# One layer of a hybrid attention and recurrence block on one core: the whole program issued from one list schedule, with twelve more pairs of weight blocks in the seven-product form

## The chip, the cores and the metric

The kernel runs on one core of one Trainium2 chip. The time is device microseconds (us) of one launch, and the figure that counts is the median over the runs. The engines are named as the profile names them: PE (TensorE, matrix products; PEld are its weight loads, which overlap), DVE (VectorE), ACT (ScalarE), POOL (GpSimd) and SP (SyncE, which issues transfers). All arithmetic is float32 or a split form of it, and a matrix product is seen in the profile as many MATMUL instructions of 128 rows by 512 columns.

## The reference

For 256 tokens of width 2048 and one layer:

```python
h = rmsnorm(x, norm1_gain[l])
proj = h @ w_in[l]                          # 2048 x 7168: q k v | q f i g
attn = chunk_band_attention(q_a, k_a, v_a, rel_bias[l])   # 8 heads, chunks of 64
attn = rmsnorm(attn, attn_out_gain[l])
rec = hgrn2_mixer(q_r, f_r, i_r, g_r, lb_all[l], grn_norm_gain[l])
x = x + concatenate([attn, rec]) @ w_out[l]               # 2048 x 2048
h2 = rmsnorm(x, norm2_gain[l])
ff = silu(h2 @ w_gate[l]) * (h2 @ w_up[l])                # two of 2048 x 5632
x = x + ff @ w_down[l]                                    # 5632 x 2048
return rmsnorm(x, final_gain)
```

Only the five large products matter for the change; the mixers between them are small.

## The kernel before

**Three products for one.** Every large product is made at float32 precision from float32r operands. A weight tile `raw` is split into `wh` (ACT, a copy into float32r, L89) and `wl` (DVE, `raw - wh`, L90); the activations are held split in the same way (`hx`, `h`, `fh`/`fl`). A product is then three MATMULs into the same PSUM bank: high by high, high by low, low by high (`Group.mul`, L337).

**Groups, pairs and kinds.** The weights come from HBM in chunks of 1 MB (128 x 2048 float32, `raw`, three buffers): one chunk is a *pair*, 2 x 2 blocks of 128 rows by 512 columns. A group computes a 256 x 1024 piece of the output and runs over pairs: 8 pairs for the input projections in natural layout, for the output projection and for each of the eleven gate and up groups (`Gated`), 22 pairs for each of the two groups of the down projection (`Down`). A pair has one of three kinds:

- `d`: eight block products, 24 MATMULs. Four blocks are split, which is two `wh` and two `wl` of 1024 columns.
- `s`: seven block products in Winograd's form, 21 MATMULs. DVE first makes four sums of weight blocks in `ta` (1024 columns, L386) and `tb` (two of 512, L387 and L388), then splits the three plain blocks and the four sums: `wl` once at 512 columns and three times at 1024. The activations need four sums of their own (`row_sums`, L291: tiles `wsa`, `wsb`, `hs`, `sf`, `sx`), made once for each pair that some group runs in this form.
- `a`: eight products, without DVE. ACT writes `low = -wh` (L356), then a transfer on the queue of POOL adds the same weights from HBM to it (L357), so that `low` becomes the low part. Such a pair has two adding transfers of 512 KB and a raw buffer of its own (`rawa`).

The four tiles `wh` and four `wl` of 1024 columns are shared by all pairs, so the split of one pair runs about one pair ahead of PE.

**Gate and up.** The first group is eight `d`; the other ten run `a4 s0 d5 s1 a6 s2 s3 d7` (L1032). After its last pair a group's eight PSUM banks are combined by DVE (`spread`, `block`), and the product of gate and up is transposed on PE and split into `fh` and `fl` (`ff_split`).

**Down.** The first group has 7 `s` pairs of 22, the second 9 (`FAST`, L1145). The sums of the activations are made two pairs at a time (`sum_pairs`) in the first three gaps between pairs, and the last three alone.

**What sets the order.** The code is written group by group: while PE runs a pair, the next one is prepared (`run_groups`). The tile framework's scheduler then moves instructions on each engine as their operands allow; a few are pinned to the program's order with `keep_in_program_order` (L219, L298, L348, L356). Buffers come from pools (`wraw`, `wsp`, `dn`, `pacc`, `paux` and others) that rotate them. All plain loads stand in one queue on SP, in the order written.

```python
    full = [("a", 4), ("s", 0), ("d", 5), ("s", 1), ("a", 6), ("s", 2), ("s", 3), ("d", 7)]
    down = [Down(g, order_of(KP, list(range(FAST if g else FAST - 2)), 1 if g else 6, 2), w_down, ...)
```

Of the kernel before, what the change touches and what calls it, by code (L numbers as in the profile page):

```python
# [7 lines left out]

F32 = mybir.dt.float32
F32R = mybir.dt.float32r  # L10
# [6 lines left out]
P = 128  # L17
S = 256
# [11 lines left out]
FAST = 9  # L30
FASTU = 4
BANKS = ("c00", "c01", "c10", "c11", "m1", "m5", "m6", "m7")
# [10 lines left out]


@with_exitstack
def hybrid_block(ctx: ExitStack, tc: tile.TileContext, x, xT, w_in, w_out, w_gu, w_down,
                 bias, gains, lbnd, fgain, out):
    nc = tc.nc

    const = ctx.enter_context(tc.tile_pool(name="const", bufs=1))  # L50
    wraw = ctx.enter_context(tc.tile_pool(name="wraw", bufs=3))
    wsp = ctx.enter_context(tc.tile_pool(name="wsp", bufs=4))
    ev = ctx.enter_context(tc.tile_pool(name="ev", bufs=2))
    act_t = ctx.enter_context(tc.tile_pool(name="act_t", bufs=1))
    res = ctx.enter_context(tc.tile_pool(name="res", bufs=1))
    small = ctx.enter_context(tc.tile_pool(name="small", bufs=2))
    pacc = ctx.enter_context(tc.tile_pool(name="pacc", bufs=4, space=PSUM))
    paux = ctx.enter_context(tc.tile_pool(name="paux", bufs=4, space=PSUM))
# [22 lines left out]

    def dma(o, i):
        with ExitStack() as st:
            if prev:
                st.enter_context(tc.issue_after(prev[-1]))
            prev.append(nc.sync.dma_start(o, i).ins)

# [8 lines left out]
    def rstd_of(sums, n, cnt, tag, space=None):  # L96
        if space is None:
            space = small.tile([P, 3, n], F32, tag=tag, name=tag)
# [23 lines left out]
    def split_chunk(raw, kn, wn, pieces=1):  # L122
        parts = []
        for hf in range(2):
            wh = wsp.tile([P, 2 * W], F32R, tag="wh", name="wh")
            wl = wsp.tile([P, 2 * W], F32R, tag="wl", name="wl")
# [8 lines left out]
    def load_chunk(src, idx, pieces=1):  # L135
        raw = wraw.tile([P, KC * W], F32, tag="raw", name="raw")
# [5 lines left out]
    def tr_product(src, chunk, rhs):  # L142
        ps = [pacc.tile([P, 2, S], F32, tag="acc", name="acc") for _ in range(2)]
# [15 lines left out]
    def tr_evac(dst, ps, rows, pool, bufs=2):  # L159
        for m in range(2):  # L160
            tb = pool.tile([P, S], F32, tag="tb", name="tb", bufs=bufs)
# [4 lines left out]
    dn = ctx.enter_context(tc.tile_pool(name="dn", bufs=1))  # L166
    wsa = tc.tile_pool(name="wsa", bufs=1)
    own = {"wsa": wsa.__enter__().tile([P, 2, 4, 2, P], F32R, name="wsa")}
    mix = tc.tile_pool(name="mix", bufs=1)
    mixp = mix.__enter__()  # L170
    ab = tc.tile_pool(name="ab", bufs=1)
    abp = ab.__enter__()

    def t4(shape, name):
        return abp.tile(shape, F32, tag="t4", name=name, bufs=NT4)

    hx = act_t.tile([P, KD, 2, S], F32R, tag="hx", name="hx")
    xr = [t4([P, 4, S], "xr") for _ in range(4)]
    nc.gpsimd.memset(ones, 1.0 / 1024.0)
    wm = paux.tile([P, P], F32, tag="aux", name="wm")  # L180
# [4 lines left out]
    make_identity(nc, ident)  # L185
# [6 lines left out]
    aT = []  # L192
    for t in range(NT):
        a = abp.tile([P, 4, P], F32, name=f"aT{t}")
        nc.gpsimd.memset(a, 0.0)
        aT.append(a)
# [12 lines left out]
    ma = mixp.tile([P, 2, 8, S], F32R, name="ma")  # L209
    kx = mixp.tile([P, 2, 2, 4, S], F32R, tag="mr", name="kx")  # L210
    rst1 = const.tile([P, NT], F32, name="rst1")
    G = res.tile([P, H, 384], F32, tag="res", name="G")
# [3 lines left out]
    def x_squares(c):  # L216
        sq = t4([P, 4, S], "sq")
        k = 0 if c else 1
        tc.keep_in_program_order(nc.scalar.activation(sq[:, k:4, :], xr[c][:, k:4, :], AF.Square))  # L219
# [9 lines left out]
    def row_rstd(dst, cols):  # L229
        pr = paux.tile([P, S], F32, tag="aux", name="prow")  # L230
        for t in range(NT):
            dg = ev.tile([P, P], F32, tag="junk", name="dg")
# [4 lines left out]
    def first_rstd():  # L237
        pr = paux.tile([P, NT], F32, tag="aux", name="pr1")
# [5 lines left out]
    def lower_bound():  # L244
        mx = small.tile([P, H], F32, tag="lbm", name="lbm", bufs=1)
        e = small.tile([P, 2, H], F32, tag="lbe", name="lbe")
# [22 lines left out]
    def transposed(nm, dst):  # L269
        tr_evac(dst, tr_product(w_in, chunk_of(nm), hx), R1, abp)  # L270
# [20 lines left out]
    def row_sums(dst, hi, lo, in_order=False):  # L291
# [5 lines left out]
        if in_order:  # L297
            tc.keep_in_program_order(first)  # L298
# [930 lines left out]
```

## Time and profile before

| | |
|---|---|
| three runs, us | 1131.49, 1131.65, 1132.62; median 1131.65 |
| span of the profiled execution | 1129.3 us, 14420 instructions |
| PE busy | 1119.4 us (99%) |
| PE weight loads busy | 936.2 us (83%) |
| DVE busy | 986.8 us (87%) |
| ACT busy | 724.1 us (64%) |
| POOL busy | 45.9 us (4%) |
| read from HBM | 245.92 MB |

The span runs from the first to the last instruction of the one execution that was profiled; the runs are timed from outside, and their median is 2.35 us above that span. No time of the profiled execution other than its span is given. By the first products that read their operands, the output projection begins at about 335 us, gate and up at about 426 us and the down projection at 891 us; the last product ends at 1121 us. Before them lie the input projections with the two mixers. A busy time is the union of an engine's instructions with their latencies, so an instruction that starts before the one ahead of it has ended is not counted twice, and the distance between two starts is less than one duration.

### The profile page before, as it was taken

How to read it: one execution, taken by the hardware profiler on the slowest of the kernel's cores; microseconds unless marked ns; L12 is line 12 of the kernel's file. 1: busy time of each engine (PE TensorE's matmuls, PEld its weight loads, DVE VectorE, ACT ScalarE, POOL GpSimd, SP SyncE). 2: the span in 40 equal slices, each digit the busy share in tenths (PEclk: the TensorE clock that was granted, in tenths of full speed). 3: DMA queues.
4: the chain of work that ended last, by engine and by line, in shares of the span. 5: the costliest groups of instructions: out<-in, count | busy, mean ns of one | idle time of the engine just before them, and what ended most of it. 6: DMA issues, size and time to landing. Idle time of an engine off the chain costs nothing.

```text
span 1129.3 us, 14420 instructions
## 1 busy us (share of the span) xinstructions
PE 1119.4 (99%) x5344; PEld 936.2 (83%) x5344; DVE 986.8 (87%) x1294; ACT 724.1 (64%) x930; POOL 45.9 (4%) x73
## 2 busy tenths in 40 slices
PE   9999999999999999999999999999999999999997
PEld 7888888888888888888888888888888888888885
DVE  7867778996999998789989989989989999898986
ACT  8555566575866666676676676676766565555563
POOL 0000000000000000000000010010010000000000
PEclk9999999999999999999999999999999999999999
DMA  8665544656455668778778878788788755655652
GB/s 337 217 214 186 185 149 150 223 191 257 149 187 187 223 203 319 223 223 229 268 251 240 266 244 251 263 238 258 250 244 252 289 192 216 223 187 190 220 189 109
DMA packets 40246, 251.05 MB, mean 222 GB/s; under 512 B 4592, under 2 KB 5104, under 8 KB 13424
## 3 DMA queue, kind: packets, MB, share of 16 engines
q1 hardware_dynamic: 32832, 220.51, 53.3%
q0 software_dynamic: 7200, 29.36, 13.4%
q8 instruction: 42, 0.69, 0.2%
q10 hardware_dynamic: 144, 0.26, 0.1%
q14 instruction: 28, 0.23, 0.1%
HBM read 245.92 MB, written 4.19 MB: 221 GB/s over the span
## 4 chain that ended last, share of the span: by engine, by line
PE 96%; DVE 2%; ACT 1%; DMA 0%; issue 0%; SPq 0%; ACTq 0%
PE c L337 62%; PE m L337 16%; PE acc L151 11%; PE acc L154 5%; PE ptr L282 1%; DVE wl L90 1%; PE po L793 0%; PE pa L766 0%; DMA GX<-in_gains_dram 0%; ACT wh L89 0%; PE pp L518 0%; DVE oo L807 0%; PE po L795 0%; PE pc L773 0%; PE sc L498 0%
## 5 line engine op out<-in xcount | busy, mean ns | idle before, releaser
L89 ACT ACTIVATE wh<-raw 128x1024 fp32r<-128x1024 f32 (+1 forms) x368 | 351.7, 971 | 182.1 <-PE c L337 84.1
L90 DVE TENSOR_TENSOR wl<-raw,wh 128x1024 fp32r<-128x1024 f32 (+1 forms) x368 | 403.4, 1113 | 72.6 <-ACT wh L89 71.6
L337 PE MATMUL c<-wh,h 128*128 128x512 f32 x928 | 274.2, 390 | 0.0
L337 PEld LDWEIGHTS c<-wh,h 128*128 128x128 f32 x928 | 174.2, 188 | 36.6 <-DVE ff L1011 0.3
L151 PE MATMUL acc<-hx,wh 128*128 128x512 f32 x512 | 162.2, 397 | 0.0
L89 ACT ACTIVATE wh<-ta 128x1024 fp32r<-128x1024 f32 x66 | 70.1, 1061 | 88.0 <-PE c L337 46.3
L337 PE MATMUL c<-wl,h 128*128 128x512 f32 x304 | 119.4, 393 | 0.0
L89 ACT ACTIVATE wh<-tb 128x1024 fp32r<-128x1024 f32 x66 | 70.0, 1061 | 71.0 <-PE c L337 38.8
L154 PEld LDWEIGHTS acc<-hx,wl 128*128 128x128 f32 x512 | 96.2, 188 | 22.5
L337 PE MATMUL c<-wh,hx 128*128 128x512 f32 x336 | 105.5, 392 | 0.2 <-DVE hx L628 0.2
L154 PE MATMUL acc<-hx,wl 128*128 128x256 f32 x512 | 100.7, 278 | 0.0
L90 DVE TENSOR_TENSOR wl<-ta,wh 128x1024 fp32r<-128x1024 f32 x66 | 80.7, 1223 | 18.8 <-ACT wh L89 18.8
L90 DVE TENSOR_TENSOR wl<-tb,wh 128x1024 fp32r<-128x1024 f32 x66 | 80.6, 1222 | 11.8 <-ACT wh L89 9.2
L337 PE MATMUL c<-wh,fh 128*128 128x512 f32 x224 | 87.3, 390 | 0.2 <-DVE ff L1003 0.2
L337 PE MATMUL c<-wh,fl 128*128 128x512 f32 x224 | 87.2, 389 | 0.0
L337 PE MATMUL c<-wl,fh 128*128 128x512 f32 x224 | 87.1, 389 | 0.0
L386 DVE TENSOR_TENSOR ta<-raw 128x1024 f32<-128x1024 f32 x66 | 80.7, 1222 | 1.7 <-DMA raw<-in_w_down_dram 0.9
L337 PE MATMUL m<-wh,hs 128*128 128x512 f32 x240 | 81.8, 389 | 0.0
L151 PEld LDWEIGHTS acc<-hx,wh 128*128 128x128 f32 x512 | 78.4, 189 | 0.1
L337 PEld LDWEIGHTS c<-wh,hx 128*128 128x128 f32 x336 | 63.2, 188 | 13.6 <-ACT wh L89 0.5
L337 PEld LDWEIGHTS c<-wl,h 128*128 128x128 f32 x304 | 57.1, 188 | 14.0 <-DVE wl L90 2.5
L337 PE MATMUL c<-wl,hx 128*128 128x512 f32 x168 | 64.8, 391 | 0.0
(353 smaller groups left out, 1730.9 us busy)
## 6 DMA issues: line engine op xcount, KB each, us to landing
raw<-in_w_gu_dram SPq DMA_DIRECT2D x68, 1024.0 KB, 6.8
raw<-in_w_in_dram SPq DMA_DIRECT2D x54, 1024.0 KB, 4.8
raw<-in_w_down_dram SPq DMA_DIRECT2D x44, 1024.0 KB, 4.8
rawa<-in_w_gu_dram SPq DMA_DIRECT2D x20, 1024.0 KB, 6.1
low<-in_w_gu_dram POOLq DMA_DIRECT2D x40, 512.0 KB, 6.9
raw<-in_w_out_dram SPq DMA_DIRECT2D x14, 1024.0 KB, 4.8
x<-in_x_dram SPq DMA_DIRECT2D x2, 1024.0 KB, 7.9
rawa<-in_w_out_dram POOLq DMA_DIRECT2D x2, 1024.0 KB, 7.1
```

The lines of the kernel that those rows point to most:

```text
L89: nc.scalar.activation(hi, src, AF.Copy)
L90: nc.vector.tensor_tensor(lo, src, hi.bitcast(F32), ALU.subtract)
L151: nc.tensor.matmul(ps[m].rearrange("p j t -> p (j t)"), lhsT=wh[:, cols[m]], rhs=both, start=kt == 0, stop=False)
L154: nc.tensor.matmul(ps[m][:, 0, :], lhsT=wl[:, cols[m]], rhs=rhs[:, kt, 0, :], start=False, stop=kt == KD - 1)
L282: nc.tensor.transpose(pt[:, j, t, :], nat(t)[:, n0 + j * P:n0 + (j + 1) * P], ident)
L337: nc.tensor.matmul(self.bank[n], lhsT=a, rhs=b, start=self.left[n] == self.total[n], stop=self.left[n] == 1)
L386: nc.vector.tensor_tensor(ta, raw[:, 1:3], raw[:, 0:2], ALU.subtract)
```

## The change

**One list schedule.** All operations from the first memset of `aT` on are no longer issued as the code runs. Stand-ins for the engines (`Taken`) record each in a list (`Plan.add`) with an estimated duration and with the places that it reads and writes. When the list is complete, `Plan.order` plays it through at build time: PE takes the first ready one of the next 48 in its list, DVE and ACT the ready one that is due first (counted back from the end), SP and POOL keep the order written. The program is then issued in the order of these starts with the framework's own scheduler off (`manual_schedule`). Buffers are no longer drawn from pools but from fixed places (`Places`, `fixed`, `turn`).

**Five raw buffers.** From the output projection to the end of gate and up, `raw0` to `raw2` are joined by two more of 1 MB, `more`; `rawa` is gone. The down projection has three again.

**More seven-product pairs.** A new kind `b` is the seven-product form in which the low part of the two plain blocks `b22` and `b21` is made by one adding transfer as in `a`, instead of by DVE. Gate and up groups 1 to 8 run `a5 s0 b1 s2 a6 s3 b4 d7`: five seven-product pairs and six adding transfers instead of four and four. Group 9 has five seven-product pairs and four transfers, group 10 four and none. A fifth pair's activation sums are kept in the still empty end of `fh` (`hs5`), and the added low parts go to `low`, of which there is one buffer, and to the still empty ends of `fh` and `fl`. That is 9 more pairs. In the down projection 9 and 10 pairs instead of 7 and 9 are of the form, 3 more. There the activation sums are made one pair at a time (`sum_pair`), the fourth sum in the place of a block that the pair no longer needs.

```diff
+    def add(self, engine, what, emit, out, ins, kind="w", own=(), func=None):
+        busy, done = self.cost(engine, what, out, ins, func)
...
+        self.ops.append((engine, busy, done, size, emit, set(), func if func in self.OWN else None, touched))
...
+        with self.tc.manual_schedule(engines={E.PE, E.DVE, E.Activation, E.Pool}):
+            for i in self.order():
+                self.ops[i][4]()
...
+            b22, b21 = self.added_half(raw, low, 1) if kind == "b" else halves_of(raw[:, 2:4])
...
         def prepare(i):
             gr, n = todo[i]
-            nxt, m = todo[i + 1] if i + 1 < len(todo) else (None, 0)
-            begins = nxt is not None and nxt.items[m][0] == "a"
-            if begins:
-                nxt.begin(nxt.items[m][1])
-                nxt.lower(0)
...
+            kind, j = gr.items[n]
+            if kind in "ab":
+                gr.begin_ahead(j)
+            for k in {"a": (0, 1), "b": (1,)}.get(kind, ()):
+                gr.lower(j, k)
+            return gr.prepare(kind, j)
...
+                fixed["raw"] += [new(f"more{i}", [P, KC * W], F32, "more") for i in range(2)]
...
-    full = [("a", 4), ("s", 0), ("d", 5), ("s", 1), ("a", 6), ("s", 2), ("s", 3), ("d", 7)]
+    orders = ["d0 d1 d2 d3 d4 d5 d6 d7"] + 8 * ["a5 s0 b1 s2 a6 s3 b4 d7"] + ["a5 s0 b1 s2 b3 s4 d6 d7", "d4 s0 d5 s1 d6 s2 s3 d7"]
...
-        def sum_pairs(self, j, n):
-            ks, js = slice(2 * j, 2 * j + 2 * n), slice(j % 2, j % 2 + n)
-            row_sums((sf[:, j // 2] if j < FAST - 1 else own["sx"])[:, :, :, js, :], fh[:, ks, :], fl[:, ks, :])
+        def sum_pair(self, j):
+            ks = slice(2 * j, 2 * j + 2)
+            s, k = (sf, j) if j < FAST - 1 else (own["sx"], 0)
+            ff = turn("ff")
+            sm = form_sums(fh[:, ks, :], fl[:, ks, :], ff[:, 0].rearrange("p (a b c) -> p a b c", a=1, b=2),
+                           ff[:, 1].rearrange("p (a b c) -> p a b c", a=4, b=1))
+            split(s[:, 0, :, k, :], s[:, 1, :, k, :], sm[:, 0:3, 0])
+            split(fh[:, 2 * j, P:S], fl[:, 2 * j, P:S], sm[:, 3, 0])
...
-    down = [Down(g, order_of(KP, list(range(FAST if g else FAST - 2)), 1 if g else 6, 2), w_down, g * KP, f_of, s_of)
-            for g in range(2)]
+    kinds = "ddd" + 9 * "sd" + "d", "d" + 8 * "sd" + "ssddd"
+    down = [Down(g, fast_first(kinds[g]), w_down, g * KP, f_of, s_of) for g in range(2)]
```

Over the whole program the built instructions change as follows: PE has 4394 MATMULs of 512 columns instead of 4430, the shorter ones are the same; DVE has 1380 instructions instead of 1292, among them 42 more of 512 columns, 6 more of 1024, 42 more of 128, 10 more of 384 and 12 fewer of 256; ACT has 21 more of 1024 columns, 30 more that are shorter and 22 loads of a function table instead of 17; POOL issues 56 adding transfers instead of 44. In the changed program nearly all rows carry line 336, that of the stand-in, so the tiles tell them apart; `bank` is a PSUM bank.

**How it moves on ACT in a gate and up group.** Before, both `low` of an `a` pair (tile `low`, from `rawa`) are written shortly before the pair's own high parts (`wh<-rawa`):

```order
L992 COPY ff<-m_6544 128x512
L356 ACTIVATE low<-rawa 128x1024
L89 ACTIVATE wh<-raw 128x1024 x2
L356 ACTIVATE low<-rawa 128x1024
L366 ACTIVATE wh<-rawa 128x1024 x2
L1009 ACTIVATE ff<-ff,rst_2804 128x512
```

Now the low parts (tiles `fl`, `low` and `fh` by where they are kept, from `raw` or `more`) stand singly among the splits of pairs that come earlier:

```order
L336 ACTIVATE wh_80<-more 128x1024
L336 ACTIVATE fl<-raw_76 128x1024
L336 ACTIVATE wh_82<-tb 128x1024
L336 ACTIVATE fl<-raw_76 128x1024
L336 ACTIVATE wh_79<-more 128x512
L336 ACTIVATE wh_80<-more 128x1024
L336 ACTIVATE wh_81<-ta 128x1024
L336 ACTIVATE wh_82<-tb 128x1024
L336 ACTIVATE wh_79<-raw_78 128x1024
L336 ACTIVATE wh_80<-raw_78 128x1024
L336 COPY ff<-bank_95 128x512
L336 ACTIVATE wh_81<-raw_76 128x1024
```

The two `fl` are one `a` pair's; ten other ACT instructions and more now stand between them and the pair's high parts, so an adding transfer is issued two to three pairs before it is used.

**How it moves on DVE at the start of the down projection.** Before, the activation sums (`a`, `sm`, then the low part `sf`) of two pairs at a time stand among the splits of `d` pairs, whose only DVE work is `wl<-raw,wh`:

```order
L295 TENSOR_TENSOR a<-fh,fl 128x1024
L90 TENSOR_TENSOR wl<-raw,wh 128x1024
L300 TENSOR_TENSOR sm<-a 128x256
L302 TENSOR_TENSOR sm<-a 128x256
L301 TENSOR_TENSOR sm<-sm,a 128x256
L303 TENSOR_TENSOR sm<-a,sm 128x256
L295 TENSOR_TENSOR a<-fh,fl 128x1024
L90 TENSOR_TENSOR sf<-sm,sf 128x1024
L90 TENSOR_TENSOR wl<-raw,wh 128x1024
```

Now the sums of one pair (in `ff`) are laid singly between the steps of an `s` pair (`tb` and the first two of its four `wl`):

```order
L336 TENSOR_TENSOR wl_83<-raw_76,wh_79 128x512
L336 TENSOR_TENSOR ff<-ff 128x128
L336 TENSOR_TENSOR tb<-raw_76,ta 128x512
L336 TENSOR_TENSOR ff<-ff 128x128
L336 TENSOR_TENSOR tb<-raw_76,tb 128x512
L336 TENSOR_TENSOR wl_84<-raw_76,wh_80 128x1024
L336 TENSOR_TENSOR fl<-ff,fh 128x128
L336 TENSOR_TENSOR ff<-ff 128x128
```

The sums have moved from the stretch of `d` pairs into the stretch where `s` and `d` alternate, and nine sets stand there one by one instead of four.

More of the change, by code (lines that the diff above doesn't have):

```diff
@@ L45, in hybrid_block, with __init__ @@
+class Engines:
+    def __init__(self, plan, nc):
+        self.tensor, self.vector, self.scalar = (Taken(plan, e, n) for e, n in ((nc.tensor, "PE"), (nc.vector, "DVE"), (nc.scalar, "ACT")))
+        self.gpsimd, self.sync = Taken(plan, nc.gpsimd, "POOL"), Taken(plan, nc.sync, "SP")
 @with_exitstack
@@ L86, in dma @@
             prev.append(nc.sync.dma_start(o, i).ins)
+    half = scratch = turn
     def split(hi, lo, src):
@@ L353, in lower, with begin_ahead, low_tile @@
-        def lower(self, k):
-            j, raw, low = self.begun
-            wl = own["low"].tile([P, 2, W], F32R, tag="low", name="low", bufs=3)
-            tc.keep_in_program_order(nc.scalar.activation(wl, raw[:, 2 * k:2 * k + 2], AF.Copy, scale=-1.0))
+        def begin_ahead(self, j):
+            if j not in self.begun:
+                self.begun[j] = load_chunk(self.src, self.base + j).rearrange("p (b n) -> p b n", n=W), {}
+        def low_tile(self):
+            return turn("low")
```

646 lines of the change are left out of this document (483 added, 163 removed).

## The prediction

> **What bounds the kernel now.** I read the page's busy shares first, then the busy times of single stages, the chain of work in one gate and up group, the waits, and last the transfers of a group.
>
> ```profile
> PE 1119.4 (99%) x5344; PEld 936.2 (83%) x5344; DVE 986.8 (87%) x1294; ACT 724.1 (64%) x930; POOL 45.9 (4%) x73
> ...
> PE 96%; DVE 2%; ACT 1%; DMA 0%; issue 0%; SPq 0%; ACTq 0%
> ```
>
> PE is busy all the time and is 96% of the chain that ended last. Whether it could go faster shows in the distance of its products on that chain.
>
> ```profile
> 616.44 2.04 PE m L337 x9
> 618.48 6.12 PE c L337 x27
> ```
>
> 27 products follow each other in 6.12 us, 0.2267 us each, and the next piece begins where the last ended. At this distance PE has no gap to give, and only fewer products shorten it.
>
> ```profile
> L337 PEld LDWEIGHTS c<-wh,h 128*128 128x128 f32 x928 | 174.2, 188 | 36.6 <-DVE ff L1011 0.3
> ```
>
> [...]
>
> Next, who waits for whom, and how much of each engine a stage uses (rows: window, then busy time of PE, PEld, DVE, ACT, POOL with counts, PE clock, DMA share, GB/s).
>
> ```profile
> ACT wh L89 <- PE c L337: 169.2, 169, 3.8
> ...
> DVE wl L90 <- ACT wh L89: 99.7, 130, 1.9
> ```
>
> ```profile
> 0.00:45.00 45.00, 43.69 (x190) 36.08 (x191) 36.41 (x61) 31.11 (x46) 3.13 (x17) 1.00 0.82 305
> ...
> 292.60:334.40 41.80, 41.80 (x195) 34.78 (x194) 40.49 (x54) 30.37 (x36) 0.00 (x0) 1.00 0.55 193
> 326.00:363.00 37.00, 36.88 (x199) 31.19 (x198) 35.93 (x63) 24.14 (x42) 0.67 (x1) 1.00 0.53 185
> ...
> 604.86:646.76 41.90, 41.90 (x189) 34.53 (x189) 38.50 (x45) 29.01 (x34) 3.48 (x4) 1.00 0.81 251
> ...
> 891.03:1006.60 115.57, 115.57 (x514) 95.77 (x515) 107.03 (x124) 66.10 (x75) 0.00 (x0) 1.00 0.63 225
> 1006.60:1120.80 114.20, 114.20 (x515) 94.73 (x514) 103.12 (x129) 64.83 (x77) 0.00 (x0) 1.00 0.50 178
> ```
>
> ACT waits for PE to free `wh`, DVE for ACT: the queue stands in front of PE. The clock is full in every stage. DVE is close behind: 92% in a gate and up group (604.86), 93% and 90% in the two down groups, 97% at 292.60, where PE was still unbroken.
>
> **1. Products.** Twelve pairs lose 3 products each: 36 x 0.2267 = **-8.2 us**. All lie on the chain. A gate and up group with a fifth such pair shrinks from 41.9 to 41.2 us, the first down group by six products from 115.6 to 114.2, the second by three to 113.5.
>
> **2. DVE.** A pipelined DVE instruction holds the engine less than its duration; the distances are read where starts follow each other (start, us, then the group).
>
> ```profile
> 303.20 0.69 DVE L90 TENSOR_TENSOR wl<-raw,wh 128x512 fp32r<-128x512 f32 x1
> 303.80 1.22 DVE L734 TENSOR_TENSOR kdec<-kdec,kk 128x1024 f32<-128x1024 f32 x1
> 304.94 1.22 DVE L90 TENSOR_TENSOR wl<-raw,wh 128x1024 fp32r<-128x1024 f32 x1
> 306.07 1.22 DVE L90 TENSOR_TENSOR wl<-ta,wh 128x1024 fp32r<-128x1024 f32 x1
> 307.21 0.42 DVE L742 COPY kf<-kdec 128x512 f32<-128x512 f32 x1
> 307.54 0.42 DVE L744 TENSOR_TENSOR ks<-kdec,eb 128x256 f32<-128x256 f32 x1
> 307.88 0.29 DVE L746 COPY ks<-kdec 128x256 f32<-128x256 f32 x1
> 308.08 1.22 DVE L90 TENSOR_TENSOR wl<-tb,wh 128x1024 fp32r<-128x1024 f32 x1
> ```
>
> That is 1.135 us for 1024 columns, 0.60 for 512, 0.34 for 256 and 0.20 for 128; for 384 I take 0.47, between its neighbours. A pair `s` is four of 1024 and three of 512: 6.3 us; `b` one of 1024 fewer, 5.2; `d` two of 1024, 2.3; `a` none.
>
> A gate and up group now is 20 of 1024 and, with the evacuation, 24 of 512: 37.1 us at these distances (the 38.50 hold some latency besides). Groups 1 to 8 get three more of 512: 38.9 of 41.2 us. Group 9 is 22 and 27: 41.2 of 41.2. Group 10, without `a`, is 24 and 24: 41.6 of 41.9. The first down group is 104.4 us of distances now (65, 43, 12 and 4 instructions of 1024, 512, 256 and 128 columns stand in its window). Two pairs turn from `d` to `s`: +8.1. The activation sums are now three double sets of 3.6 and a single one of 2.0, then nine single sets of 2.07 (one of 512, five of 128, one of 384): +5.8. That makes 118.3 against PE's 114.2.
>
> So groups 1 to 8 cost nothing, since the row at 292.60 carries 97% without a gap. Groups 9, 10 and the first down group together ask DVE for 201.1 us in PE's 197.3: **3.8 us too many**. What may slip into the second down group, which gains one `s` and loses one set (+2.1) and has some 8 us free, are the products with the final gain (four of 512, 2.4 us) and the last two additions to `x2` (1.2). The lower end is then 0.2 us. For the upper end, DVE's own waits of this stage today come on top:
>
> ```profile
> L386 DVE TENSOR_TENSOR ta<-raw 128x1024 f32<-128x1024 f32 x8 | 9.8, 1223 | 1.0 <-DMA raw<-in_w_down_dram 0.9
> L90 DVE TENSOR_TENSOR wl<-tb,wh 128x1024 fp32r<-128x1024 f32 x7 | 8.6, 1224 | 3.0 <-ACT wh L89 2.9
> L90 DVE TENSOR_TENSOR wl<-ta,wh 128x1024 fp32r<-128x1024 f32 x7 | 8.6, 1224 | 3.6 <-ACT wh L89 3.6
> ```
>
> These are 7.6 us: 11.4 in all. They are mostly ACT waiting for PE's `wh` and should go when DVE is the late one, as at 292.60. I take **+1.2**, near the lower end.
>
> **3. Transfers.** In the gate and up group of 604.86 (41.90 us; queue, packets, MB, share of the 16 engines):
>
> ```profile
> q1 hardware_dynamic: 1152, 8.39, 51.6%
> q0 software_dynamic: 576, 2.10, 29.7%
> ...
> raw<-in_w_gu_dram SPq DMA_DIRECT2D x6, 1024.0 KB, 6.7
> low<-in_w_gu_dram POOLq DMA_DIRECT2D x4, 512.0 KB, 6.2
> ```
>
> Eight loads take 21.6 us, four adding transfers 12.4, 3.1 each. With six it is 40.3 of 41.2 us: the idle part falls from 7.9 to 0.9 us per group. Five raw buffers and adding transfers issued two to three pairs ahead let both queues run on. I count 0; the ends are 0 and the second rival. POOL issues 4 in 3.48 us, 6 would be 5.2. An adding transfer waits on POOL for ACT's `low` and for its place to be read; behind it stand only other adding transfers. ACT in turn stands on a `low` whose `raw` has not landed, and then the splits behind it wait, which DVE and PE need within a pair: that is how a late load would be felt. SP's queue has two loads more, the output projection's that POOL issued.
>
> ```profile
> raw<-in_w_down_dram SPq DMA_DIRECT2D x21, 1024.0 KB, 4.8
> ```
>
> A load lands in 6.7 us here and in 4.8 in the down projection, where nothing is added. [...]
>
> **4. Mixers, head, tail.** Five more table loads on ACT at 1.283 each are 6.4 us, spread over a part where ACT is busy 24.14 of 37.00: 0, at most 6.4.
>
> ```profile
> 0.81 1.28 ACT L184 ACT_TABLE_LOAD   x1 [0.81 <-PEq L1217]
> ...
> 5.09 39.29 PE c L337 x168
> ...
> 1120.82 0.28 PE L1064 MATMUL half<-wh,f_last 128*128 128x256 f32 x1
> ```
>
> The first product at 5.09 us waits for the same loads in the same order, and the last 8 us have the same chain: 0. In the head PE has 1.3 us of gaps (43.69 of 45.00), which another order might close or widen by as much.
>
> **Sum.** -8.2 + 1.2 = -7.0. From the span of 1129.3 us this gives 1122.3; the median of the runs is 2.35 above that span, so **1124.7**.
>
> **Rivals.** (a) *DVE keeps its waits in the down projection*: with all 11.4 us the time is 1134.9, with half of the waits (3.8 + 3.8) 1131.1, no change. For it speaks that the first down group has no slack at all, against it the row at 292.60. (b) *Transfers become the wall of gate and up*, the slower side: each of the 8 groups takes 40.3 us plus what the DMA engines stand idle. Today that is 7.9 us; above 0.9 PE waits, at 1.8 the gain of 7.0 is used up, at 2.5 us idle the 8 groups cost 8 x 1.6 = 12.8: 1137.5, slower. For it: the share of 0.81 would have to reach 0.98, and no row here shows that over 40 us. Against: the present idle stretches come with three buffers and late `low`. (c) *The changed order puts the table loads where PE waits*: 1131.1; ACT has room, and DVE is the dense engine there.
>
> **Chances.** Forecast (1122 to 1128) 0.82; (a) 0.07, (b) 0.07, (c) 0.04. A measurement here tells about 0.2% from no change, 2.3 us. Of (a) 0.02 is still faster and 0.05 no change; (b) is slower in 0.05 and no change in 0.02; (c) is no change. So faster 0.84, same 0.11, slower 0.05. The range goes down to 1121.5 (all 8.2 us, DVE's 0.2, and the 1.3 of the head closed, 1122.4, with a little over) and up to 1130, into (a).
>
> **What would show it.** Right: products at 0.2267 with PE at 99%, a middle gate and up group of 41.2 us, the first down group of about 115.4, DVE above 95% in it. Step 2 is wrong if PE waits for `wl` there by over 4 us; step 3 if a group takes 42 us and PE or ACT waits for `low`, `fl`, `fh` or `raw`; step 4 if PE has gaps between 50 and 330 us. The whole is wrong if DMA share stays near 0.9 in gate and up while the group does not shrink.

## The result and the profile after

The changed kernel takes 1144.77 us, median of six runs (1139.35 to 1146.21); the kernel before took 1131.88 beside it (1131.34 to 1132.8). The ratio is 1.0103, 95% interval 1.0082 to 1.0124: 1.0% slower, where 0.6% faster was forecast. Six further runs of the same kernel gave 1142.15 and 1.0089 (1.0073 to 1.0105). The profiled execution is the quickest of its six, with a span of 1137.6 us.

From the page of the kernel after, busy times and the chain that ended last:

```profile
PE 1122.0 (99%) x5308; PEld 927.4 (82%) x5308; DVE 1023.0 (90%) x1382; ACT 756.9 (67%) x986; POOL 54.7 (5%) x83
...
PE 86%; DVE 7%; DMA 3%; ACT 2%; issue 2%; SPq 0%; ACTq 0%; DVEq 0%
```

PE has 36 instructions fewer than before and is busy 2.6 us longer. Busy shares hide what happened, as both kernels show 99%. What tells is how many products fit into a stretch without a gap. A window in the second down group, before and then after (window, busy time and count of PE, PEld, DVE, ACT, POOL; PE clock, DMA share, GB/s):

```profile
1005.00:1100.00 95.00, 95.00 (x421) 78.67 (x420) 87.57 (x101) 58.16 (x67) 0.00 (x0) 1.00 0.57 199
```

```profile
1005.00:1100.00 95.00, 95.00 (x417) 77.93 (x416) 90.81 (x105) 54.20 (x64) 0.00 (x0) 1.00 0.57 203
```

PE is unbroken in both and the clock is full in both, and yet four products fewer fit in. The chain of the input projection says the same, far from any dense engine: before (start us, us, what)

```profile
205.96 7.71 PE c L337 x34
```

and after

```profile
205.79 32.27 PE bank L336 x141
```

That is 226.8 against 228.9 ns for one product. Read from the starts, the unbroken stretches in which PE loads activations as weights have 226.67 ns in the kernel before and 228.9 in the changed kernel, from the head to the last group. The 512 products of 512 columns in which activations move (those for q and k of the attention and q and f of the recurrence, where products of 512 and of 256 columns alternate) go the other way: two of each take 697 ns before and 694 after. DVE's distances are the same in both (1.135 us for 1024 columns).

The second loss is in gate and up. A window over its middle, before and then after:

```profile
500.00:800.00 300.00, 300.00 (x1348) 247.47 (x1347) 275.21 (x315) 208.51 (x238) 24.43 (x29) 1.00 0.81 250
```

```profile
500.00:800.00 300.00, 300.00 (x1329) 242.85 (x1328) 287.98 (x337) 229.72 (x264) 36.94 (x43) 1.00 0.95 277
```

The DMA engines are busy 95% over 300 us. What ACT waits for there (us in total, times, longest us), from the waits of the kernel after between 428 and 890 us:

```profile
ACT fl L336 <- DMA raw<-in_w_gu_dram: 5.3, 3, 2.7
ACT low L336 <- DMA more<-in_w_gu_dram: 3.2, 2, 1.9
ACT low L336 <- DMA raw<-in_w_gu_dram: 3.2, 3, 1.2
```

and the longest wait of PE in it:

```profile
PE bank L336 <- DMA fl<-in_w_gu_dram: 1.7, 1, 1.7
```

In the same stretch of the kernel before neither engine has such a row among its longest waits. ACT's three rows, 11.7 us together, are not the mark of full queues, though: the run below with all pairs of before, whose DMA share is 0.82, has 11.4 us of them.

The third is in the mixers. PE stands there once:

```profile
202.98 0.51 PE L336 MATMUL bank<-wh,hx 128*128 128x512 f32 x1 [1.80 <-DVE parts L336]
```

The bank that it needs is emptied by a copy on ACT and an addition on DVE (timeline of ACT, then of DVE):

```profile
198.26 1.28 ACT L336 ACT_TABLE_LOAD   x1 [0.80 <-DVE ma L336]
199.55 1.06 ACT L336 ACTIVATE kinv<-bb 128x1024 f32<-128x1024 f32 x1
200.52 0.62 ACT L336 COPY parts<-bank 128x256 f32<-128x256 f32 x2
```

```profile
200.23 1.22 DVE L336 TENSOR_TENSOR kdec<-bb 128x1024 f32<-128x1024 f32 x1
201.37 1.22 DVE L336 TENSOR_TENSOR kinv<-kinv,kk 128x1024 f32<-128x1024 f32 x1
202.50 0.75 DVE L336 TENSOR_TENSOR parts<-bank,parts 128x256 f32<-128x256 f32 x2
```

A table load, which itself waited 0.80 us, and `kinv` stand ahead of the copy, and two instructions of 1.14 us each ahead of the addition.

### The profile page after: what moved, and what is told of

Read it like the earlier page. It is cut to its first block, busy times and chain, and to the rows that moved or that the text cites. A ratio compares the mean times of both kernels' runs of the same rounds, so it can differ in the third digit from the quotient of the medians.

```text
span 1137.6 us, 14463 instructions
## 1 busy us (share of the span) xinstructions
PE 1122.0 (99%) x5308; PEld 927.4 (82%) x5308; DVE 1023.0 (90%) x1382; ACT 756.9 (67%) x986; POOL 54.7 (5%) x83
## 4 chain that ended last, share of the span: by engine, by line
PE 86%; DVE 7%; DMA 3%; ACT 2%; issue 2%; SPq 0%; ACTq 0%; DVEq 0%
PE bank L336 86%; DVE wl L336 3%; DMA raw<-in_w_gu_dram 1%; DMA fl<-in_w_gu_dram 1%; ACT wh L336 1%; DVE x L336 1%; DVE ta L336 1%; DMA xr<-in_xT_dram 0%; DVE tb L336 0%; DVE ra L336 0%; DVE at L336 0%; SPq L336 0%; DVE hs L336 0%; ACT junk L336 0%; DVE fin L336 0%
## 5 line engine op out<-in xcount | busy, mean ns | idle before, releaser
L336 PE MATMUL bank<-wh,h 128*128 128x512 f32 x918 | 281.5, 394 | 1.2 <-ACT ff L336 1.2
L336 PEld LDWEIGHTS bank<-wh,h 128*128 128x128 f32 x918 | 172.1, 188 | 40.4 <-ACT ff L336 1.6
L336 PE MATMUL bank<-hx,wh 128*128 128x512 f32 x512 | 161.1, 395 | 0.0
L336 PE MATMUL bank<-wh,fh 128*128 128x512 f32 x316 | 120.2, 392 | 0.0
L336 PE MATMUL bank<-wl,h 128*128 128x512 f32 x305 | 117.5, 391 | 0.0
L336 PEld LDWEIGHTS bank<-hx,wl 128*128 128x128 f32 x512 | 96.1, 188 | 21.6
L336 PE MATMUL bank<-wh,hx 128*128 128x512 f32 x344 | 108.7, 393 | 2.1 <-DVE parts L336 1.8
L336 PE MATMUL bank<-wh,hs 128*128 128x512 f32 x320 | 108.0, 395 | 0.0
L336 PE MATMUL bank<-wl,fh 128*128 128x512 f32 x272 | 106.2, 393 | 0.0
L336 DVE TENSOR_TENSOR wl<-ta,wh 128x1024 fp32r<-128x1024 f32 x78 | 95.1, 1220 | 11.7 <-ACT wh L336 11.4
L336 PE MATMUL bank<-hx,wl 128*128 128x256 f32 x512 | 101.2, 279 | 0.0
```

What stands on the lines that cost most here:

```text
L336: return call(*[real(a) for a in args], **{k: real(v) for k, v in kw.items()})
```

## The experiments

The kernel before ran beside each of them, with a median of 1131.6 to 1131.9; the last column is the ratio to it with its 95% interval. Diffs are against the changed kernel, and every run that has "64 bytes" in its row contains the first diff as well.

| run | median us | lowest to highest | ratio |
|---|---|---|---|
| changed kernel, first time | 1144.77 | 1139.35 to 1146.21 | 1.0103 (1.0082 to 1.0124) |
| changed kernel, second time | 1142.15 | 1137.91 to 1145.02 | 1.0089 (1.0073 to 1.0105) |
| 64 bytes in the changed kernel | 1137.6 | 1136.18 to 1139.09 | 1.0052 (1.0039 to 1.0064) |
| 32 bytes ahead of `raw0` | 1139.68 | 1138.97 to 1140.35 | 1.0069 (1.0054 to 1.0085) |
| 64 bytes in the kernel before | 1151.42 | 1151.22 to 1151.75 | 1.0173 (1.0159 to 1.0187) |
| 64 bytes, adding transfers halved | 1130.48 | 1129.89 to 1132.58 | 0.9992 (0.9983 to 1.0001) |
| 64 bytes, five adding transfers | 1135.26 | 1134.29 to 1135.89 | 1.0033 (1.0020 to 1.0045) |
| 64 bytes, five and four in turn | 1135.34 | 1133.74 to 1136.93 | 1.0030 (1.0019 to 1.0040) |
| 64 bytes, four transfers, four pairs | 1134.8 | 1133.28 to 1137.19 | 1.0028 (1.0017 to 1.0040) |
| 64 bytes, four transfers, five pairs | 1140.94 | 1140.15 to 1141.18 | 1.0079 (1.0065 to 1.0093) |
| 64 bytes, all pairs of before | 1136.4 | 1134.55 to 1139.02 | 1.0037 (1.0023 to 1.0051) |
| four and four, banks due earlier | 1138.08 | 1136.78 to 1138.41, and once 2914.3 | 1.0052 (1.0038 to 1.0066) |

The one time of 2914.3 is left out of its ratio. The runs were spread over several chips: the changed kernel with 64 bytes and with 32 ran on one chip, its second round without them on another.

The time from the first transpose of `ff` in one gate and up group to that in the next, us, for the ten intervals of each run's profiled execution; the last column is the sum of the first eight, which are groups 1 to 8:

```
before                 41.9 41.9 41.9 41.9 41.9 41.9 41.9 41.9 41.9 42.2   335.0
after                  42.2 41.6 41.8 41.7 41.6 41.9 42.2 43.9 41.7 42.3   336.9
64 bytes               41.9 41.5 41.7 41.6 42.7 43.1 41.6 42.9 41.4 42.1   336.9
 + transfers halved    41.4 41.8 41.6 41.5 41.4 41.5 42.5 41.7 41.8 41.9   333.3
 + five transfers      41.3 41.5 41.3 41.3 41.3 41.3 43.0 41.7 43.7 41.9   332.8
 + five and four       41.3 43.8 41.6 41.9 41.6 41.9 41.7 41.8 41.9 41.9   335.5
 + four, four pairs    41.7 41.8 41.9 41.8 41.9 41.9 41.8 42.0 41.9 41.9   334.7
 + four, five pairs    41.2 43.0 42.0 42.5 42.5 42.4 42.9 42.5 43.9 41.9   339.0
 + all pairs of before 42.1 45.4 41.9 41.9 41.7 41.9 41.9 41.9 41.9 42.2   338.7
```

### 64 bytes in the changed kernel

```diff
     for n in ("ta", "tb"):
         fixed[n] = [place.tile([P, 2, W], F32, name=n)]
+    tc.nc.gpsimd.memset(place.tile([P, 16], F32, name="pad"), 0.0)
```

> The changed kernel with one unused tile of 64 bytes per partition between `tb` and everything behind it. The activations (the operand that PE loads as weights: `hx`, `h`, `hs`, `fh`, `fl`, `sf`, `f_last`) then begin at 32 modulo 128 bytes again, as in the kernel before, instead of at 96; `wh` and `wl` stay at 32. Nothing else changes, so the order is the same. Theory A (place): the distance of two products follows from where these operands begin; it goes from 228.9 ns back to 226.67 in every unbroken stretch, 4394 x 2.22 = 9.8 us less: profiled span near 1128, median 1135. Rival B (order): the distance comes from the list schedule's order on PE, which mixes banks and operands; then it stays at 228.9 and the median at 1144.8. Rival C (state of the chip or of one launch): a distance that varies from run to run, with no relation to the tile.

```profile
1005.00:1100.00 95.00, 95.00 (x420) 78.39 (x419) 90.56 (x105) 53.32 (x63) 0.00 (x0) 1.00 0.59 213
```

The distance is back at 226.67 ns in the stretches that had 228.9, with the same order on PE: rivals B and C fall. The 9.8 us did not come. The span of the profiled execution falls by 3.2 us, to 1134.4, and none of that lies in gate and up groups 1 to 8, which take 336.9 us in both executions: waits fill there what the shorter distance frees. The median is 4.5 and 7.2 us below the changed kernel's two, but with another chip on the other side, and not all of that is the distance, as the next run shows.

### 32 bytes ahead of the raw buffers

```diff
+    tc.nc.gpsimd.memset(place.tile([P, 8], F32, name="pad"), 0.0)
     fixed = {}
     for n, count, dt in (("raw", 3, F32), ("wh", 4, F32R), ("wl", 4, F32R)):
```

> The changed kernel with an unused tile of 32 bytes per partition ahead of `raw0`: `wh` and `wl` then begin at 64 modulo 128 and the activations at 0. Theory A1 (only the place of the weight operand counts, and 0 or 32 are good, 96 is bad): 226.67 ns or less, median 1135 or less. A2 (both operands have to begin in the same half of 128 bytes: 32 and 32 were good, 32 and 96 bad): still 228.9, median 1144.8. Rival B (order): still 228.9. If 226.67 is set by something else than place, 0 gives no distance below it.

```profile
1005.00:1100.00 95.00, 95.00 (x417) 77.94 (x416) 90.81 (x105) 54.45 (x64) 0.00 (x0) 1.00 0.57 202
```

228.9 ns: A1 falls and A2 holds. It is not where the activations begin, but where they begin in relation to the moving operand. (PE loads the activations as weights; `wh` and `wl` move through it.) The median is 2.1 us above the 64-byte run's on the same chip. It is also 2.5 and 5.1 us below the changed kernel's, with the same distance and the same order on PE; no run explains that difference.

### 64 bytes in the kernel before

```diff
+    pad = ctx.enter_context(tc.tile_pool(name="pad", bufs=1))
+    nc.gpsimd.memset(pad.tile([P, 16], F32, name="pad"), 0.0)
     ev = ctx.enter_context(tc.tile_pool(name="ev", bufs=2))
```

> The kernel before with an unused tile of 64 bytes per partition behind the weight tiles: its activations move from 32 to 96 modulo 128, the weights stay at 32; order and work are those of before. Theory A (place): 228.9 ns instead of 226.67, 4430 x 2.22 = 9.8 us more, median 1141.7. Rival B (order): 226.67 and 1131.9 as before.

```profile
1005.00:1100.00 95.00, 95.00 (x409) 76.14 (x408) 89.19 (x104) 53.44 (x62) 0.00 (x0) 1.00 0.55 193
```

1151.42: an idle tile of 64 bytes costs this kernel 19.6 us, 1.7%, with not one instruction moved. The sign was as expected, the size twice as large: 233.33 ns, not 228.9. So a modulus of 128 was too coarse. (6.7 ns on the 3918 products that load activations would be 26 us; not all of it shows in the time.) By the addresses of the build `hx` begins 0 above `wh` modulo 256 before, 192 above it in the changed kernel and in the 32-byte run, and 64 above it here.

### The distance by itself

```python
for mov in (mova, movb):            # 512 columns each; movb begins 64 bytes higher modulo 256
    for w in ws:                    # wa to wp, each begins 32 bytes higher modulo 256 than the last
        for i in range(30):
            nc.tensor.matmul(banks[b % 7], lhsT=w[:, 0:P], rhs=mov, start=i == 0, stop=i == 29)
        b += 1
```

> A measurement by itself, which leaves out the whole layer: two moving tiles of 512 columns (`mova` at 128, `movb` at 192 modulo 256 bytes) and sixteen weight tiles `wa` to `wp`, whose beginnings step by 32 bytes modulo 256; for each of the 32 combinations 30 products stand one behind the other. The runs so far have three distances: 226.67 ns where the weight operand begins at the same place modulo 256 as the moving one, 233.33 where it begins 64 higher, 228.89 where 192 higher. Theory A2 (only the difference modulo 256 counts): here the same three values, for both moving tiles, `wa` (64) at 233.33 and `we` (192) at 228.89 with `mova`, and each value again 8 tiles on; 0 for `mova` is `wg`, for `movb` `wa`. If contention with DVE, ACT or transfers is needed, all are 226.67 here. If some other difference lies below 226.67, a faster place exists for every product of the layer.

Timeline of PE for the first moving tile (start us, us, what); the difference of two starts is 30 products:

```profile
29.17 7.16 PE L43 MATMUL bank<-mova,wa 128*128 128x512 f32 x30
36.17 7.18 PE L43 MATMUL bank<-mova,wb 128*128 128x512 f32 x30
43.19 7.13 PE L43 MATMUL bank<-mova,wc 128*128 128x512 f32 x30
50.16 7.17 PE L43 MATMUL bank<-mova,wd 128*128 128x512 f32 x30
57.16 7.04 PE L43 MATMUL bank<-mova,we 128*128 128x512 f32 x30
64.05 7.17 PE L43 MATMUL bank<-mova,wf 128*128 128x512 f32 x30
71.05 7.00 PE L43 MATMUL bank<-mova,wg 128*128 128x512 f32 x30
77.89 7.15 PE L43 MATMUL bank<-mova,wh 128*128 128x512 f32 x30
84.88 7.16 PE L43 MATMUL bank<-mova,wi 128*128 128x512 f32 x30
```

| weights begin above the moving tile, modulo 256 | 0 (`wg`) | 32 | 64 | 96 | 128 | 160 | 192 (`we`) | 224 |
|---|---|---|---|---|---|---|---|---|
| 30 products, us | 6.84 | 6.99 | 7.00 | 7.02 | 6.97 | 7.00 | 6.89 | 7.00 |
| one, ns | 228.0 | 233.0 | 233.3 | 234.0 | 232.3 | 233.3 | 229.7 | 233.3 |

In the long unbroken stretches above, 0 has 226.7 and 192 has 228.9; I put the 0.02 to 0.04 us that the 30 products take beyond these down to the change of tile, which is an estimate. Each value comes again 8 tiles on, and the second moving tile gives the same by difference: with `movb` the shortest are `wa` (the first of that row) and `wi`. Apart from one addition on DVE and one output transfer that begin with `wa`, no other engine works in this time, so it is no contention with DVE, ACT or transfers. No difference is below 0: for such a stream the kernel before already had the best place. For the alternating products it had not: two of 512 and two of 256 columns take 697 ns there and in the 64-byte run, 694 in the changed kernel and the 32-byte run, and 691 with 64 bytes in the kernel before. The rule by difference is one for unbroken products of 512 columns.

### The changed kernel again

No edit.

> The changed kernel once more, on one chip beside the others. Its first six runs lay between 1139.35 and 1146.21; the 32-byte run, whose products have the same distance of 228.89, lay between 1138.97 and 1140.35. Theory U (the spread belongs to the chip that ran it, or to the phase of transfers at launch): 1139 to 1141 or again up to 1146, without a change in the distance. If the place of the operands set the spread, it is up to 1146 here too.

1137.91 to 1145.02, and the profiled run again has 228.9: the spread is not in the products. All twelve runs of this kernel lie within 8.3 us, those of the kernel before within 2.3. Full DMA queues alone do not make it: the 64-byte and 32-byte runs, with the same DMA share of 0.95, lie within 2.9 and 1.4 us, the run with halved transfers (below), at 0.81, within 2.7, and the one with all pairs of before, at 0.82, within 4.5. What makes the spread stays open, the chip included.

### Adding transfers halved

```diff
                 real = self.plan.places.real
+                if "accum_op" in kw:
+                    kw = dict(kw, out=real(kw["out"])[:, 0:W], in_=kw["in_"][:, 0:W])
```

> The 64-byte run, where each adding transfer moves and adds only the first 512 of its 1024 columns; the other half of those low parts stays -wh, which is left out of the computation. Orders, products, ACT and DVE work are the same to the instruction; the DMA engines lose some 9 us of work in a group of 41.2. Theory T (the queues are full, so loads land late and ACT, then PE, waits): the groups take 41.2 each, gate and up loses its gaps and the time falls by 7 to 9 us, 1137.6 to about 1129.5. Rival L (the order of the list schedule, the few places for low parts or the fixed latency of an adding transfer make PE wait): 1136 or more.

The same window of the 64-byte run and of this one:

```profile
500.00:800.00 300.00, 298.84 (x1324) 241.14 (x1324) 287.54 (x337) 228.91 (x265) 37.02 (x43) 1.00 0.95 275
500.00:800.00 300.00, 299.65 (x1333) 242.68 (x1332) 288.08 (x338) 230.86 (x266) 36.93 (x43) 1.00 0.81 240
```

1130.48, 7.1 us below the 64-byte run: theory T, as far as the price goes. DVE and ACT are as busy as there, only the DMA share fell, from 0.95 to 0.81. Of the 3.9 us between the two profiled spans 3.6 lie in groups 1 to 8. The groups come to 41.4 to 41.8 with one of 42.5, not to 41.2. By which wait the bytes reach PE is not shown: a shorter adding transfer lands earlier itself (into `fl` after 5.5 us instead of 7.8), and loads land earlier beside it too (into `raw` after 6.5 instead of 7.3, into `more` after 5.5 instead of 7.0). What weight loads still wait for in gate and up:

```profile
PEld bank L338 <- DVE wl L338: 4.2, 14, 0.6
PEld bank L338 <- DVE fl L338: 4.1, 14, 0.5
```

### Four adding transfers, four pairs

```diff
-    orders = ... + 8 * ["a5 s0 b1 s2 a6 s3 b4 d7"] + ...
+    orders = ... + 8 * ["a4 s0 d5 s1 a6 s2 s3 d7"] + ...
```

> As the 64-byte run, and gate and up groups 1 to 8 take the pair kinds of the kernel before (four seven-product pairs and four adding transfers instead of five and six): 24 products more, 5.4 us. Theory T (six adding transfers a group cost PE about 5 us of waits in most runs, and make the runs differ by 7 us): median equal to the 64-byte run within 1.5 us, and the runs lie within 2 us of each other. Rival S (the rest of the loss is the list schedule itself, in the mixers and at the group boundaries): 5.4 us slower than the 64-byte run, and the spread stays.

1134.8: 2.8 us faster than with six although PE has 24 products more, and the groups are even at 41.7 to 42.0. T is right in direction and missed both its numbers: the gain is more than 1.5, and the runs still spread over 3.9 us. The fifth pair with its two transfers costs 2.8 + 5.4 = 8.2 us of waits, more than it gives; DVE has less to do here too, so the 8.2 are not the transfers' alone. Loads and adding transfers in gate and up, issue to landing in us, for six transfers (changed kernel) and then for four:

```profile
raw<-in_w_gu_dram SPq DMA_DIRECT2D x49, 1024.0 KB, 7.3
more<-in_w_gu_dram SPq DMA_DIRECT2D x34, 1024.0 KB, 7.0
fl<-in_w_gu_dram POOLq DMA_DIRECT2D x26, 512.0 KB, 8.4
```

```profile
raw<-in_w_gu_dram SPq DMA_DIRECT2D x49, 1024.0 KB, 5.0
more<-in_w_gu_dram SPq DMA_DIRECT2D x34, 1024.0 KB, 5.0
fl<-in_w_gu_dram POOLq DMA_DIRECT2D x18, 512.0 KB, 5.7
```

Loads and most adding transfers land later at a share of 0.95 than at 0.83, those into `low` too (8.6 and 5.5); those into `fh` go the other way (7.6 and 11.3).

### Five adding transfers

```diff
-    orders = ... + 8 * ["a5 s0 b1 s2 a6 s3 b4 d7"] + ...
+    orders = ... + 8 * ["a5 s0 b1 s2 a6 s3 s4 d7"] + ...
```

> As the 64-byte run, and one of the six adding transfers of gate and up groups 1 to 8 is taken back: `b4` becomes `s4`, five seven-product pairs stay. By the rows of before the DMA engines then have 4.1 us to spare in a group of 41.2 instead of 0.9, and DVE has 40.0 us of distances in 41.2. Theory T (the adding transfers are late because the queues are full): most of the 8 us that the fourth run won by two transfers fewer comes back with one fewer: 1137.6 - 5 to 8 = 1129.5 to 1132.5, below before or level with it. Rival D (DVE is the limit of a group with five seven-product pairs): no gain, 1137 or more, and PE waits for `wl`.

```profile
500.00:800.00 300.00, 298.61 (x1334) 243.23 (x1334) 292.83 (x343) 226.35 (x259) 31.81 (x37) 1.00 0.88 264
```

1135.26, a gain of 2.3, between what T (5 to 8) and D (none) had. Six groups reach 41.3 to 41.5, near the 41.2 that the prediction wanted of all. Then intervals of 43.0 and, in group 9, of 43.7 take it back, the first when PE waits 1.1 us for an adding transfer into `fh`. DVE is at 98% here.

### Five and four in turn

```diff
-    orders = ... + 8 * ["a5 s0 b1 s2 a6 s3 b4 d7"] + ...
+    orders = ... + 4 * ["a5 s0 b1 s2 a6 s3 s4 d7", "a4 s0 d5 s1 a6 s2 s3 d7"] + ...
```

> As the 64-byte run, with gate and up groups 1 to 8 in turn of five adding transfers and five seven-product pairs, and of four and four. In the run with five transfers in each group six groups took 41.3 us and then three took 41.7 to 43.7. Theory E (arrears: the queues fall behind a little in each group, the buffers cover it for some, and a group of four pays it back): no stumble, groups of 41.3 and 41.9 in turn, and 12 products fewer than with four in each: 1134.8 - 2.7 = 1132.1. Rival (any group with five transfers can stumble, whatever comes before): 1134.5 or more.

The late stumbles are gone, as theory E has it, and from the third on the intervals lie at 41.6 to 41.9. But the time is 1135.34, as the rival had it, and in the profiled execution the second interval took 43.8: PE stood 1.9 us at 528.7, for DVE's `fl`. The same gap stands in the profile with all pairs of before. Arrears fit the later groups; the gain was lost elsewhere, and the run does not decide it.

### Four adding transfers, five pairs

```diff
-    orders = ... + 8 * ["a5 s0 b1 s2 a6 s3 b4 d7"] + ...
+    orders = ... + 8 * ["a5 s0 s1 s2 a6 s3 s4 d7"] + ...
```

> As the 64-byte run, with both `b` of gate and up groups 1 to 8 turned into `s`: five seven-product pairs, but four adding transfers; DVE gets two more instructions of 1024 columns, 41.2 us of distances in a group of 41.2. If a full DVE carries a group without gaps (as the second step of the prediction took for groups 9 and 10), the groups take 41.2 and the time is 1134.8 - 5.4 = 1129.4. Rival D (a DVE without slack delays PE): groups of 42 us or more, 1135 to 1140, and PE waits for `wl`.

```profile
500.00:800.00 300.00, 297.06 (x1309) 237.49 (x1308) 291.84 (x343) 217.41 (x246) 23.98 (x28) 1.00 0.80 245
```

The DMA engines are as free as before and DVE is at 97%; it takes 1140.94, and after the first interval groups of 42.0 to 43.9. That is rival D, and weight loads wait for DVE or for what stands behind it (the last row: ACT's `wh` waits for DVE's `wl`, which in the 64-byte run it does for 15.9 us):

```profile
PEld bank L336 <- ACT wh L336: 8.2, 19, 1.1
PEld bank L336 <- DVE fl L336: 3.8, 7, 1.6
PEld bank L336 <- DVE wl L336: 3.0, 9, 0.7
ACT wh L336 <- DVE wl L336: 29.5, 41, 2.0
```

For two of its blocks a fifth pair needs 1.14 us of DVE twice or an adding transfer twice, and a group has room for neither.

### All pairs of before under the list schedule

```diff
-    orders = ... + 8 * ["a5 s0 b1 s2 a6 s3 b4 d7"] + ["a5 s0 b1 s2 b3 s4 d6 d7", "d4 s0 d5 s1 d6 s2 s3 d7"]
+    orders = ... + 8 * ["a4 s0 d5 s1 a6 s2 s3 d7"] + 2 * ["d4 s0 d5 s1 d6 s2 s3 d7"]
-    kinds = "ddd" + 9 * "sd" + "d", "d" + 8 * "sd" + "ssddd"
+    kinds = "dddddd" + 7 * "sd" + "dd", "d" + 9 * "sd" + "ddd"
```

> The list schedule with the work of before: the 64-byte tile, four adding transfers and four seven-product pairs in gate and up groups 1 to 8, four pairs and no transfer in groups 9 and 10, 7 and 9 pairs in the down projection; 4430 products of 512 columns as before. Theory S (the list schedule itself costs 5 to 6 us: 1.5 in the head, 2 in the mixers, the rest in small waits): 1131.6 + 5.5 = 1137, within 1.5. Rival P (the four pairs more of the four-transfer run make the waits on DVE, in groups 9 and 10 and the down projection): no more than 1134.8, since the 2.7 us of their products are offset by the waits that go.

1136.4, 4.7 us slower than before with the same products at the same distance: theory S, a little under its number. The gap at 203 us stands here too, with 1.9 us. The profiled execution is the slowest of the five, 2.6 us above their median, with one interval of 45.4 us in gate and up. Counted product by product against the kernel before, it is 1.0 us behind at 45 us, 2.8 just after the gap at 203, and 4.1 when gate and up begins (429.7 against 425.6).

### Banks due earlier

```diff
             late[i] = min([late[k] - 50 for k in after[i] ...] + [0.0]) - done
+            if e in ("DVE", "ACT") and any(kind == "r" and ap.tensor.name.startswith("bank") for ap, kind in ops[i][7]):
+                late[i] -= 2000
```

> As the run with four adding transfers, and the list schedule counts DVE and ACT instructions that read a PSUM bank as due 2 us earlier, so that on DVE `parts<-bank` and its like go ahead of `kdec` and `kinv`. In all list-scheduled runs PE stands 1.9 us at 203 us, where DVE does 2 x 1.13 us of these first, and 0.9 at 356. Theory S (the order of DVE around the emptying of banks costs what the four-transfer run loses in the mixers): the gap at 203 falls below 0.3 us and the time by 2 to 3 us, 1134.8 to about 1132. Rival: the gap only moves to another place, and the time stays within 1 us.

This diff is on top of the four-transfer run. It is 3.3 us slower than that (1138.08), as neither theory had it, and the gap at 203 is unchanged at 1.9 us. My reading of it fell: due times do not matter there. When ACT came free the copy was not yet possible, as PE had not ended the bank; the list schedule then gave ACT what was ready, a table load and `kinv`, and never lets an engine wait for something better. That is how the rows read; no run forced the other order. The waits for DVE in the down projection grew instead.

## Why the prediction was wrong

Each of these kernels differs from the one above it in one respect, or nearly so (the third has six transfers of half size, the second four whole ones). A line is a difference of two medians from different chips, and the intervals of the ratios leave 1 to 2.4 us to either side of each median:

| step | us against the line above |
|---|---|
| kernel before | 1131.7 |
| list schedule, pairs of before, 64 bytes | +4.7 |
| twelve more pairs, six transfers a group, but halved | -5.9 |
| the transfers whole | +7.1 |
| without the 64 bytes: the changed kernel | +4.5 to +7.2 |

Three terms of the sum failed. The distance of products was taken as 0.2267 us and is 0.2289; the transfers were put at 0 and cost 7.1; the new order was put at 0 and costs 4.7.

**1. Products.** The count was right (36 fewer), the distance was not: "0.2267 us each" was read from the kernel before and carried over. The changed kernel draws its tiles from fixed places, which moved the activations by 192 modulo 256 against `wh` and `wl`, and the 3882 remaining products of 512 columns that load activations cost 2.2 ns more each, +8.6 us; the 512 in which activations move give 0.7 us back. In the time it is 2.1 us between the 32-byte and the 64-byte run on one chip and 3.2 between two profiled spans; the 4.5 to 7.2 of the table hold more than the distance, and what else is open. This is the failed step with no term at all in the sum. The move of the tiles stood in the description of the change, and I took it to be free. The measurement by itself shows what place alone does: 6.84 to 7.02 us for 30 products.

**2. DVE.** For the first down group it was right. From its first product to the next group's the 64-byte run takes 115.4 us, the predicted 115.4, and the changed kernel 115.8 (by these marks the kernel before takes 115.9, where the prediction's window gave 115.57, so the exact hit is partly luck). DVE has no slack there and PE no gap, as the same stretch of the changed kernel shows:

```profile
899.34:1015.15 115.81, 115.81 (x511) 94.70 (x509) 115.25 (x169) 71.13 (x92) 0.00 (x0) 1.00 0.62 223
```

So rival (a) did not come. In gate and up the step failed in part: "groups 1 to 8 cost nothing" since one row carried 97% without a gap. With halved transfers they still lost 0.2 to 0.6 us each, one of them 1.3, with weight loads waiting for `wl` and `fl`; with five pairs and four transfers, DVE at 97%, they took 42.0 to 43.0 after the first. One stretch of 42 us does not show what an engine carries for 300. All the same the twelve pairs gave 5.9 of the 7.0 us that the sum had for them.

**3. Transfers.** Counted 0 and it was 7.1 us: rival (b), which got 0.07. Its working was good. At a share of 0.95 a group of 42.1 us, the mean of the 64-byte run, has 2.1 us idle, so 40.3 + 2.1 = 42.4, and eight groups cost 8 x 1.2 = 9.6 against 41.2. Wrong was what kept its chance low, that no row showed a share of 0.98 and that five buffers let both queues run on. The queues came to 0.95, and PE already waited. The two landings that the prediction compared, 6.7 and 4.8 us, also say little about what adding transfers do to a load: under the list schedule, with four of them a group, loads landed after 5.0. I had set the limit to 0.9 us idle myself, and should have asked what leaves less than 2% idle.

**4. Mixers, head, tail.** Counted 0, and the list schedule costs 4.7 us without any new pair. Of the 4.1 us by which its profiled execution is late into gate and up, 1.0 is lost in the head, inside the 1.3 that the prediction allowed, and 1.9 in the gap at 203 us, as the rows read by a table load ahead of a bank's copy: rival (c) at one place, not at five. The rest lies in gaps below a microsecond up to the end of the output projection (0.9 at 356 us), and no run took it apart. That another order of the same work is free was never worked out from a row.

The mistakes went one way: terms stood at zero because something covered them. Two covers, DVE's 2.3 us and the queues' 0.9 us in a group, were read from single stretches of some 40 us and spent over eight groups. Two more, the places and the order, were read from no row at all.

No version here beats the kernel before. The halved transfers come to 0.9992 (0.9983 to 1.0001) and leave work out.

## What to carry to other kernels

Before comparing orders, compare the distance of two products in an unbroken stretch: if it differs at full clock, look at where the two operands begin modulo 256 bytes, and pad until they begin alike (here 226.7 ns alike, 228.9 to 234 otherwise). That holds for unbroken streams of equal products; here alternating ones had another best place. A plan that fills DVE or the queues to 95% or more over hundreds of microseconds should be priced as late, not as covered (here the queues at 0.95 over 300 us, against 0.81, cost 7.1 us, and DVE at 97% came with groups of 42.0 to 43.9 us after a first of 41.2), and an extra transfer can cost more than the work that it saves (here a fifth pair with its two transfers came to 8.2 us of waits, not all of them the transfers', for 5.4 of products). When a change moves every tile and every instruction, give the move a term of its own, and test it with the old work under the new order.

## What the runs showed of the hardware

In an unbroken stream, a product of 128 by 512 float32r columns takes 226.7 ns when weights and moving operand begin alike modulo 256 bytes, 228.9 when the weights begin 192 higher, and about 232 to 234 at the six other multiples of 32, with the granted clock at 1.00 throughout. Where two products of 512 and two of 256 columns alternated, equal beginnings were the slowest of three: 697 ns for the four, 694 with the weights 64 above the moving operand, 691 with 192. A load of weights took 188 ns at either distance. DVE's distances did not change with the place (1.135 us for 1024 columns before and after). Under the list schedule, loads of 1 MB into `raw` landed after 7.3 us with the 16 DMA engines busy at 0.95 and after 5.0 at 0.83, adding transfers of 512 KB into `fl` after 8.4 and 5.7; in the kernel before, at 0.81, loads into `raw` landed after 6.9, so the share alone does not set it. Halving the adding transfers was worth 7.1 us of 1137.6.
